# A first load of 128 descriptors, cut into four transfers over interleaved partitions (split GELU times x2)

## The chip, the cores and the metric

The kernel runs on one core of one Trainium2 chip. The metric is device time in microseconds (us) of one execution. Before the change it is 469.26 us, the median of three runs that lie between 469.24 and 469.31 us. A profile of one execution has a span of 467.9 us, from the first to the last instruction of the core; the execution that was profiled took 469.19 us. Times inside the kernel are counted from the start of that span.

## What is computed

The input has 32 x 512 rows of 2048 float32 values. In each row the first 1024 values go through the exact GELU and are multiplied by the other 1024.

```python
batch, seq, dim = (32, 512, 2048)
x1, x2 = (x[..., :half_dim].copy(), x[..., half_dim:].copy())
gelu_x1 = 0.5 * x1 * (1 + erf(x1 / np.sqrt(2)))
return (gelu_x1 * x2).astype(np.float32)
```

So 134.22 MB are read from HBM and 67.11 MB are written to it.

## The kernel before

A tile is 128 partitions of `R = 8` rows each, 8 MB of input and 4 MB of output; there are 16 tiles, and two buffers for each side. Partition `p` of a tile holds eight neighbouring rows, so a whole tile is one run of 64 KB per partition in HBM and in SBUF, and a half tile (four rows) one run of 32 KB. An engine that issues a transfer names the partitions and rows; one transfer becomes a list of descriptors, here one for each partition, which the core's 16 DMA engines work off.

```python
R = 8
x_t = x_flat.rearrange("(n p r) d -> n p r d", p=P, r=R)
x_bufs = [nc.alloc_sbuf_tensor(f"x{k}_tile", [P, R, dim], x.dtype) for k in range(2)]
o_bufs = [nc.alloc_sbuf_tensor(f"o{k}_tile", [P, R, half], out.dtype) for k in range(2)]
first = [nc.alloc_semaphore(f"first{j}") for j in range(2)]
# ...
def load(i, rows, sem):
    ins = nc.sync.dma_start(out=x_bufs[i % 2][:, rows, :], in_=x_t[i][:, rows, :])
    counted(ins, sem, 16)
    return ins
```

Three loads are issued by SyncE ahead of everything else: tile 0 in two halves, each with a semaphore of its own, and tile 1 whole. They are not put off behind the barrier that `tc.close()` ends with.

```python
for ins in (
    load(0, slice(0, 4), first[0]),
    load(0, slice(4, 8), first[1]),
    load(1, slice(0, 8), ready[1]),
):
    tc.no_tile_sem_insts.add(ins.ins.name)
tc.close()
```

Then, for each tile, ScalarE waits for the load, computes the GELU of the first half of each row into the output buffer, and VectorE multiplies it by the other half. The first and the last tile go in pieces of 2, 2 and 4 rows, the others in 5 and 3. The store is issued by ScalarE's queue (the last ones by SyncE's), and the load of tile `i + 2` by SyncE as soon as tile `i` has been multiplied. A load and the store of the same buffer number share the semaphore `ready[k]`, which ScalarE waits for two tiles later.

```python
for i in range(n_tiles):
    k = i % 2
    # ...
    for lo, hi in steps:
        rows = slice(lo, hi)
        if i == 0 and lo % 4 == 0:
            nc.scalar.wait_ge(first[lo // 4], 16)
        elif lo == 0:
            nc.scalar.wait_ge(ready[k], n[ready[k].name])
        # ScalarE: activation GELU; VectorE: tensor_mul; stores
    # ...
    if i + 2 < n_tiles:
        nc.sync.wait_ge(mul_done, n[mul_done.name])
        load(i + 2, slice(0, R), ready[k])
```

Of the kernel before, what the change touches and what calls it, by code (L numbers as in the profile page):

```python
# [1 line left out]

# [4 lines left out]

GELU = mybir.ActivationFunctionType.Gelu


@with_exitstack
def kernel(
    ctx: ExitStack,
    tc: tile.TileContext,
    x: bass.AP,
    out: bass.AP,
):
    nc = tc.nc
    P = nc.NUM_PARTITIONS

    x_flat = x.flatten_outer_dims()
    out_flat = out.flatten_outer_dims()
    n_rows, dim = x_flat.shape
    half = dim // 2

    R = 8
    x_t = x_flat.rearrange("(n p r) d -> n p r d", p=P, r=R)
    o_t = out_flat.rearrange("(n p r) d -> n p r d", p=P, r=R)
    n_tiles = x_t.shape[0]
# [6 lines that stand above are left out]
    ready = [nc.alloc_semaphore(f"ready{k}") for k in range(2)]  # L36
    gelu_done = nc.alloc_semaphore("gelu_done")
    mul_done = nc.alloc_semaphore("mul_done")
    tail_stored = nc.alloc_semaphore("tail_stored")
    n = {sem.name: 0 for sem in [*first, *ready, gelu_done, mul_done, tail_stored]}  # L40

    def counted(ins, sem, by):
        ins.then_inc(sem, by)
        n[sem.name] += by

    def load(i, rows, sem):
        ins = nc.sync.dma_start(out=x_bufs[i % 2][:, rows, :], in_=x_t[i][:, rows, :])  # L47
        counted(ins, sem, 16)
        return ins

    def store(queue, i, rows, sem):
        queue.wait_ge(mul_done, n[mul_done.name])
        counted(
            queue.dma_start(out=o_t[i][:, rows, :], in_=o_bufs[i % 2][:, rows, :]), sem, 16
        )

    for ins in (  # L60
        load(0, slice(0, 4), first[0]),
        load(0, slice(4, 8), first[1]),
        load(1, slice(0, 8), ready[1]),
    ):
        tc.no_tile_sem_insts.add(ins.ins.name)
    tc.close()
    tc.compile()  # L67

    for i in range(n_tiles):
        k = i % 2  # L70
        last = i == n_tiles - 1
        pieces = i == 0 or last
        steps = ((0, 2), (2, 4), (4, 8)) if pieces else ((0, 5), (5, 8))
        for lo, hi in steps:
            rows = slice(lo, hi)
            if i == 0 and lo % 4 == 0:
                nc.scalar.wait_ge(first[lo // 4], 16)
            elif lo == 0:
                nc.scalar.wait_ge(ready[k], n[ready[k].name])
            counted(  # L80
                nc.scalar.activation(  # L81
                    out=o_bufs[k][:, rows, :], in_=x_bufs[k][:, rows, :half], func=GELU
                ),
                gelu_done,
                1,
            )
            nc.vector.wait_ge(gelu_done, n[gelu_done.name])
            counted(
                nc.vector.tensor_mul(  # L89
                    out=o_bufs[k][:, rows, :],  # L90
                    in0=o_bufs[k][:, rows, :],
                    in1=x_bufs[k][:, rows, half:],
                ),
                mul_done,
                1,
            )
            if pieces and hi % 4 == 0:
                if last:
                    store(nc.sync, i, slice(hi - 4, hi), tail_stored)
                else:  # L100
                    store(nc.scalar, i, slice(hi - 4, hi), ready[k])
        if not pieces:
            if i == n_tiles - 2:
                store(nc.sync, i, slice(0, R), tail_stored)
            else:
                store(nc.scalar, i, slice(0, R), ready[k])
# [5 lines that stand above are left out]
    nc.scalar.drain()  # L112
    for sem in (*first, *ready):
        nc.scalar.sem_clear(sem)
    nc.vector.drain()
    nc.vector.sem_clear(gelu_done)
    nc.sync.sem_clear(mul_done)
    nc.sync.wait_ge(tail_stored, n[tail_stored.name]).then_inc(
        tail_stored, -n[tail_stored.name]
    )  # L120


# [1 line left out]
_INS = ['x']  # L124
_OUTS = [((32, 512, 1024), 'float32')]


# [23 lines left out]
```

## Time and profile before

| what | value |
|---|---|
| time, median of 3 | 469.26 us |
| span of the profile | 467.9 us |
| VectorE busy | 140.5 us (30%) |
| ScalarE busy | 115.5 us (25%) |
| DMA, mean over the span | 430 GB/s, 201.34 MB in 5041 packets |
| SyncE's queue (q1) | 2880 packets, 142.61 MB, 70.6% of 16 engines' span |
| ScalarE's queue (q10) | 2160 packets, 58.72 MB, 29.1% of 16 engines' span |
| issue of one of the first three loads | 383 to 425 ns |
| issue to landing of the first half tile | 12.0 us |
| first GELU starts at | 12.76 us |

How to read it: a page and its views give, for the core, the busy time of each engine, the DMA's share and rate in slices of the span, and the chain of waits that ended last. The window view cuts the span into stretches: each line has the length of the stretch, the busy time and number of instructions of VectorE (DVE), ScalarE (ACT) and GpSimd (POOL), a clock that does not matter here, the DMA share (1.00 is all 16 DMA engines busy) and the rate. In short windows a packet is counted whole where it starts, so the share can be over 1 in one and 0 in the next; the bytes of a window, divided by the size of a packet, count the packets that start in it. In the packet counts, each transfer of 128 descriptors has 128 data packets and 16 small ones that tell of its landing, so 144 in all.

### The profile page before, as it was taken

What the parts mean: (1) busy time and instruction counts of PE and PEld (TensorE: products, weight loads), DVE (VectorE), ACT (ScalarE), POOL (GpSimd) and SP (SyncE); (2) the same over time, 40 slices, a digit from 0 to 9 for tenths busy, and PEclk for the clock granted to TensorE, in tenths of its full rate; (3) what the DMA queues carried; (4) which work ended last, traced back from release to release, by engine and by line L of the source; (5) the groups of instructions that cost most, each with busy time, mean ns of one, the idle gap of its engine ahead of it and who ended that gap; (6) DMA issues with size and microseconds to landing.
All of it is one profiled execution on the core that took longest, in us unless ns stands there. A gap on an engine that the chain in (4) does not pass through costs nothing.

```text
span 467.9 us, 152 instructions
## 1 busy us (share of the span) xinstructions
DVE 140.5 (30%) x34; ACT 115.5 (25%) x35; POOL 0.2 (0%) x4
## 2 busy tenths in 40 slices
DVE  0330514207052060511606116060150702507043
ACT  1320606042060410604106050050500506014060
POOL 0000000000000000000000000000000000000000
DMA  8999999999999999999999999999999999999998
GB/s 359 448 448 443 403 405 492 409 403 448 459 437 403 434 417 493 403 403 448 476 420 403 445 406 493 403 406 445 487 409 403 445 451 448 403 434 417 493 389 373
DMA packets 5041, 201.34 MB, mean 430 GB/s; under 512 B 560, under 2 KB 560, under 8 KB 560
## 3 DMA queue, kind: packets, MB, share of 16 engines
q1 hardware_dynamic: 2880, 142.61, 70.6%
q10 hardware_dynamic: 2160, 58.72, 29.1%
q14 instruction: 1, 0.01, 0.0%
HBM read 134.22 MB, written 67.11 MB: 430 GB/s over the span
## 4 chain that ended last, share of the span: by engine, by line
DMA 76%; DVE 14%; ACT 8%; ACTq 0%; SPq 0%; issue 0%
DMA out_dram<-o_tile 66%; DVE o_tile L89 14%; DMA x_tile<-in_x_dram 10%; ACT o_tile L81 8%; ACTq L112 0%; SPq L47 0%
## 5 line engine op out<-in xcount | busy, mean ns | idle before, releaser
L89 DVE TENSOR_TENSOR o_tile<-o_tile,x_tile 128x5120 f32<-128x5120 f32 (+3 forms) x34 | 140.5, 4171 | 319.7 <-ACT o_tile L81 319.7
L81 ACT ACTIVATE o_tile<-x_tile 128x5120 f32<-128x5120 f32 (+3 forms) x34 | 114.3, 3407 | 337.4 <-DMA out_dram<-o_tile 301.6
L81 ACT ACT_TABLE_LOAD x1 | 1.3, 1283 | 2.9 <-PEq L67 2.9
L135 POOL MEMSET const-bfloat16-1.0<- 128x1 bf16 x1 | 0.1, 101 | 0.0
L135 POOL MEMSET const-uint8-127<- 128x1 uint8 x1 | 0.1, 101 | 0.0
L135 POOL MEMSET const-float32-0.0<- 128x1 f32 x1 | 0.1, 98 | 0.2 <-issue 0.2
L135 POOL MEMSET const-float32-1.0<- 128x1 f32 x1 | 0.1, 98 | 0.0
## 6 DMA issues: line engine op xcount, KB each, us to landing
out_dram<-o_tile ACTq DMA_DIRECT2D x13, 4096.0 KB, 44.7
x_tile<-in_x_dram SPq DMA_DIRECT2D x2, 4096.0 KB, 16.6
out_dram<-o_tile ACTq DMA_DIRECT2D x2, 2048.0 KB, 34.5
out_dram<-o_tile SPq DMA_DIRECT2D x1, 4096.0 KB, 25.2
out_dram<-o_tile SPq DMA_DIRECT2D x2, 2048.0 KB, 7.8
x_tile<-in_x_dram SPq DMA_DIRECT2D x15, 44.2
```

What stands on the lines that cost most here:

```text
L81: nc.scalar.activation(out=o_bufs[k][:, rows, :], in_=x_bufs[k][:, rows, :half], func=GELU),
L89: nc.vector.tensor_mul(out=o_bufs[k][:, rows, :], in0=o_bufs[k][:, rows, :], in1=x_bufs[k][:, rows, half:],),
L135: nc = _bacc.Bacc("TRN2", target_bir_lowering=False, num_devices=1)
```

## The change

The first half tile is loaded by four transfers, over the partitions 0, 8, 16, ... (16 of them), 4, 12, 20, ... (16), 2, 6, 10, ... (32) and 1, 3, 5, ... (64). Each partition is in exactly one of them, and each still is one descriptor of 32 KB. All four count on the same semaphore, so ScalarE waits for 64 in place of 16. It is for the start of the kernel: the DMA engines are to get their first descriptors from a short list, and the rest of the list is to be made while they work.

```diff
-    def load(i, rows, sem):
-        ins = nc.sync.dma_start(out=x_bufs[i % 2][:, rows, :], in_=x_t[i][:, rows, :])
+    first_parts = (slice(0, P, 8), slice(4, P, 8), slice(2, P, 4), slice(1, P, 2))
+
+    def load(i, rows, sem, parts=slice(0, P)):
+        ins = nc.sync.dma_start(out=x_bufs[i % 2][parts, rows, :], in_=x_t[i][parts, rows, :])
         counted(ins, sem, 16)
         return ins
@@
     for ins in (
-        load(0, slice(0, 4), first[0]),
+        *(load(0, slice(0, 4), first[0], parts) for parts in first_parts),
         load(0, slice(4, 8), first[1]),
         load(1, slice(0, 8), ready[1]),
     ):
@@
             if i == 0 and lo % 4 == 0:
-                nc.scalar.wait_ge(first[lo // 4], 16)
+                nc.scalar.wait_ge(first[lo // 4], n[first[lo // 4].name])
```

## The prediction

> **What bounds the kernel now.** I read the page first: the slices of the span, then the queues, then the chain of waits.
>
> ```profile
> span 467.9 us, 152 instructions
> DVE 140.5 (30%) x34; ACT 115.5 (25%) x35; POOL 0.2 (0%) x4
> DMA  8999999999999999999999999999999999999998
> q1 hardware_dynamic: 2880, 142.61, 70.6%
> q10 hardware_dynamic: 2160, 58.72, 29.1%
> DMA 76%; DVE 14%; ACT 8%; ACTq 0%; SPq 0%; issue 0%
> ```
>
> VectorE and ScalarE are idle for most of the time, and the DMA row is 9 in every slice but the first and the last. The two queues together hold the 16 DMA engines for 70.6 + 29.1 = 99.7% of the span. The chain gives 22% to VectorE and ScalarE only because it runs through them: while they work, the queues go on moving bytes. So the kernel is as long as the DMA engines need, and only three things count: when they start, whether they ever pause or slow down, and when they end.
>
> How near the floor is that? In the window view, the long middle stretch runs at full share and 432 GB/s:
>
> ```profile
> 0.00:1.74 1.74, 0.00 (x0) 0.00 (x0) 0.20 (x4) 1.00 0.00 0
> ...
> 100.00:400.00 300.00, 92.55 (x21) 78.35 (x22) 0.00 (x0) 1.00 1.00 432
> ```
>
> 201.33 MB at 432 GB/s are 466.0 us; 467.9 - 466.0 leaves 1.9 us, and the first line shows that 1.74 us of it pass before any packet starts. There is hardly a pause to remove behind the start. What is left to win is in that lead and in the first packets.
>
> **The start in detail.** Windows of 0.2 us over the first packets (the last two numbers of a line are the DMA share and GB/s):
>
> ```profile
> 1.40:1.60 0.20, 0.00 (x0) 0.00 (x0) 0.00 (x0) 1.00 0.00 0
> 1.60:1.80 0.20, 0.00 (x0) 0.00 (x0) 0.00 (x0) 1.00 2.27 655
> 1.80:2.00 0.20, 0.00 (x0) 0.00 (x0) 0.00 (x0) 1.00 4.66 1311
> 2.00:2.20 0.20, 0.00 (x0) 0.00 (x0) 0.00 (x0) 1.00 1.69 492
> 2.20:2.40 0.20, 0.00 (x0) 0.00 (x0) 0.00 (x0) 1.00 0.50 164
> ...
> 3.40:3.60 0.20, 0.00 (x0) 0.20 (x1) 0.00 (x0) 1.00 1.14 492
> 3.60:3.80 0.20, 0.00 (x0) 0.20 (x1) 0.00 (x0) 1.00 2.27 983
> 3.80:4.00 0.20, 0.00 (x0) 0.20 (x1) 0.00 (x0) 1.00 2.65 1147
> ```
>
> A packet of 32 KB counts as 164 GB/s in a window of 0.2 us. So 4, 8, 3 and 1 packets start in the four windows from 1.60 to 2.40: sixteen, one for each DMA engine, strung out over 0.6 us or so. The share gives their length: (2.27 + 4.66 + 1.69 + 0.50) x 0.2 us x 16 / 16 packets = 1.82 us each. The next wave starts between 3.40 and 4.00 (3 + 6 + 7 packets); its share gives (1.14 + 2.27 + 2.65) x 0.2 = 1.21 us each, and all later waves of the half tile look the same. So the first packet of an engine costs 0.61 us more than a steady one, and the engines are out of step by up to 0.6 us. As nothing pauses later, the engine that is last here stays late to the end.
>
> [...] No run so far shows a transfer over strided partitions.
>
> **The change, part by part.**
>
> *Issues.* One issue goes, four come. The old ones took 383 to 425 ns; three more delay what follows on SyncE by about 3 x 0.43 = 1.3 us. The second half tile is then issued at some 1.16 + 1.3 = 2.5 us and tile 1 at 2.9 us. The engines first need them after the eight waves of the first half, at about 12 us, so this is hidden. The same goes for the barrier behind the issues: the table load of ScalarE moves from 2.86 to about 4.2 us, and the first GELU waits until 12.76 us.
>
> *Feeding.* The first short list gives an engine one packet, to about 3.5 us. The second list is issued some 0.45 us after the first, the third and fourth 0.9 and 1.3 us after it; at the old 1.0 us from issue (0.73) to first packet (1.74) they are ready at 2.2, 2.6 and 3.1 us. They hold one, two and four more packets per engine, so no engine runs dry.
>
> *Landing packets.* Three more per engine, in a place where each has a share of 9 ns or less; 0.03 us at most, an estimate.
>
> *The first wave, where the gain is.* If the 0.6 us by which the sixteen starts differ come from making 128 descriptors, 16 of them should do it in an eighth: starts within about 0.1 us of each other. The last engine would gain up to 0.4 us, the mean one 0.2 us. The 0.61 us of extra length in the first packet look like the time to the first data, which a shorter list does not remove. I put the gain at 0.3 us, less 0.03: 469.26 - 0.27 = 469.0 us.
>
> [...] Eight waves would then take 2.42 us in place of 1.21: 8 x 1.21 = 9.7 us lost, less about a tenth[...]: 8.7 us. That gives 478 us. All of it would be on the path, since the DMA engines are the bound.
>
> **The rivals.**
> - *A short list starts the engines together[...]* (0.57). For it: the strung-out starts, no pause later. The partitions are also interleaved[...] and each prefix of the four lists is even. Time 468.6 to 469.2.
> - [...] (0.27). [...] Time 476 to 479.
> - [...] (0.08): two to four waves doubled, 2.4 to 4.8 us, so 471 to 474.
> - *Nothing is gained* (0.08): the starts differ for another reason than the length of the list, or the second list comes late to some engines. Time 469.2 to 469.7.
>
> **Range and chances.** The likeliest single outcome is 469.0 us. The outcomes lie in two heaps, at 469 and at 477; a range that holds 8 in 10 has to reach into the second, so I give 468.5 to 478.0. A gain over 2% (9.4 us) is not to be had, since only 1.9 us are not steady transfer. [...] So faster 0.01, within 2% 0.95, slower 0.04.
>
> **What would show each step right or wrong.** Windows of 0.2 us from 1.4 to 4.0 us: sixteen starts within one or two windows confirm the feeding step; the same spread refutes it. [...] Issue to landing of the first half tile: about 12 us or a little less in one case, near 20 us in the other, and the first GELU at 12.5 or at 21 us with it. The rate in the middle stretch should stay at 432 GB/s; if it changes, something other than the start is at work and the prediction is wrong in a way that it does not foresee.

## The result, and the profile after

The changed kernel takes 471.36 us (six runs, 471.27 to 471.47) beside 469.25 us (median of six) for the kernel before: a ratio of 1.0044, 95% interval 1.0031 to 1.0057. It is 2.1 us slower. The page of the changed kernel, in the lines that answer to those shown of the kernel before:

```profile
span 469.9 us, 155 instructions
DVE 140.5 (30%) x34; ACT 115.6 (25%) x35; POOL 0.2 (0%) x4
DMA  8999998999999999999999999999999999999989
q1 hardware_dynamic: 2928, 142.61, 70.7%
q10 hardware_dynamic: 2160, 58.72, 29.0%
DMA 75%; DVE 14%; ACT 8%; SPq 1%; ACTq 0%; issue 0%
```

The bound has not moved: the same bytes, the same two queues, 70.7 + 29.0 = 99.7% of the span again. 48 packets have come to SyncE's queue, the landing packets of three more transfers. What an average over the span cannot show is the start, so I cut it such that each window holds one wave, sixteen packets, as many as there are DMA engines. As a packet counts where it starts, share times length of the window is then the mean length of a packet, landing packets (the small ones that tell of a transfer's landing) included. The window view of the changed kernel (the last two numbers are the DMA share and GB/s):

```profile
0.00:2.10 2.10, 0.00 (x0) 0.00 (x0) 0.20 (x4) 1.00 0.00 0
2.10:4.00 1.90, 0.00 (x0) 0.00 (x0) 0.00 (x0) 1.00 1.23 276
4.00:6.00 2.00, 0.00 (x0) 0.88 (x1) 0.00 (x0) 1.00 1.20 262
6.00:8.00 2.00, 0.00 (x0) 0.41 (x1) 0.00 (x0) 1.00 0.83 262
8.00:9.50 1.50, 0.00 (x0) 0.00 (x0) 0.00 (x0) 1.00 0.81 350
9.50:10.50 1.00, 0.00 (x0) 0.00 (x0) 0.00 (x0) 1.00 1.23 524
```

and of the kernel before, cut in the same way:

```profile
1.60:3.00 1.40, 0.00 (x0) 0.14 (x1) 0.00 (x0) 1.00 1.30 374
3.00:4.50 1.50, 0.00 (x0) 1.14 (x1) 0.00 (x0) 1.00 0.81 350
4.50:5.50 1.00, 0.00 (x0) 0.00 (x0) 0.00 (x0) 1.00 1.21 524
```

Wave by wave, mean length of a packet of 32 KB:

| wave | list in the changed kernel | before | after | lost |
|---|---|---|---|---|
| 1 | 16, partitions 0, 8, ... | 1.82 us | 2.34 us | 0.52 us |
| 2 | 16, partitions 4, 12, ... | 1.21 us | 2.40 us | 1.19 us |
| 3 | 32, first packet | 1.21 us | 1.66 us | 0.45 us |
| 4 | 32, second packet | 1.21 us | 1.22 us | 0 |
| 5 on | 64 | 1.21 us | 1.23 us | 0 |

Wave 2 is the plain case: twice the length, and in the trace all sixteen packets of it take between 2.37 and 2.39 us. In wave 1 part of the doubling may be hidden behind what makes the first packets long in the kernel before as well (1.82 us); no run takes the two apart. Wave 3 is slow too: in the trace its packets take 1.89 us where they start first and 1.41 us where they start last. Engines still at work on wave 2 are at most part of the reason, as the last packet of wave 3 starts when wave 2 has just ended (7.41 us). The table sums to 2.16 us. To it comes a later start: the mean first packet starts at 2.26 us, not 1.92 (from the packets of the two traces), 0.34 us. (Five runs below also begin with the one list of 128 partitions; in their traces the mean is 1.96 to 2.02 us, so the later start is worth 0.24 to 0.34 us.) Together that is 2.5 us, and the first GELU starts 2.65 us later:

```profile
15.41 3.71 ACT L85 ACTIVATE o_tile<-x_tile 128x2048 f32<-128x2048 f32 x2 [9.00 <-DMA x_tile<-in_x_dram]
```

Not all of it reaches the end, which is 2.1 us later. The first wave of tile 1 (64 KB each) was slow in the kernel before, 2.70 us per packet, and is not in the changed one, 2.70 x 0.90 = 2.43 us, so 0.27 us come back there:

```profile
21.50:22.50 1.00, 0.00 (x0) 0.04 (x1) 0.00 (x0) 1.00 2.70 1049
```

```profile
24.10:25.00 0.90, 0.00 (x0) 0.00 (x0) 0.00 (x0) 1.00 2.70 1165
```

The first of these lines is of before, the second of after; each window has the sixteen packets of that wave. Why that wave has a cost in one and not in the other is not settled.

### The profile page after: what moved, and what is told of

Its sections match the earlier page's. It is cut to its first block, busy times and chain, and to the rows that moved or that the text cites. A ratio compares the mean times of both kernels' runs of the same rounds, so it can differ in the third digit from the quotient of the medians.

```text
span 469.9 us, 155 instructions
## 1 busy us (share of the span) xinstructions
DVE 140.5 (30%) x34; ACT 115.6 (25%) x35; POOL 0.2 (0%) x4
## 3 DMA queue, kind: packets, MB, share of 16 engines
q1 hardware_dynamic: 2928, 142.61, 70.7%
## 4 chain that ended last, share of the span: by engine, by line
DMA 75%; DVE 14%; ACT 8%; SPq 1%; ACTq 0%; issue 0%
DMA out_dram<-o_tile 66%; DVE o_tile L93 14%; DMA x_tile<-in_x_dram 10%; ACT o_tile L85 8%; SPq L51 1%; ACTq L116 0%
```

## Theories

**A, partitions.** The time of a packet depends on the partitions to which the packets under way at the same time go: some sets of partitions lengthen their packets, others do not. Call it a meeting when two packets lengthen each other in this way. Which packets meet was my assumption, and no trace shows a meeting as such: in a list of 16 with stride 8 each packet was to meet one other and take twice 1.21 us, in lists of 16 neighbours more of them, in lists of 32 with stride 4 and of 64 with stride 2 none. **B, transfers.** Each transfer more has a price: a longer issue, landing packets, an engine left without work. **C, the start.** Short lists are bad only where the engines have nothing else queued. **D, HBM.** The runs of a list of 16 lie 512 KB apart in HBM, and that distance is what is slow. **E, sixteen.** A list of 16 partitions with a stride is slow as such, whichever partitions they are; this rival was set up last, with the lists of stride 7.

## Experiments on the lists

**Three lists, none of 16.**

```diff
-first_parts = (slice(0, P, 8), slice(4, P, 8), slice(2, P, 4), slice(1, P, 2))
+first_parts = (slice(0, P, 4), slice(2, P, 4), slice(1, P, 2))
```

> Three lists (32, 32 and 64 partitions, strides 4, 4 and 2) in place of four; no list of 16. Theory A [...]: all packets of the first half tile after the first wave take about 1.21 us, none 2.4; only the later first packet (some 0.4 us after that of the kernel before) is left, so 469.3 to 469.7 us. Theory B (each transfer more costs about 0.7 us, by its longer issue, its landing packets or a starved engine): two transfers more in place of three, 470.5 to 470.8 us.

Measured: 469.72 us, ratio 1.0006 (0.9998 to 1.0014). The windows of its first three waves:

```profile
0.00:2.04 2.04, 0.00 (x0) 0.00 (x0) 0.20 (x4) 1.00 0.00 0
2.04:3.50 1.46, 0.00 (x0) 0.00 (x0) 0.00 (x0) 1.00 1.29 359
3.50:5.00 1.50, 0.00 (x0) 0.47 (x1) 0.00 (x0) 1.00 0.82 350
5.00:6.00 1.00, 0.00 (x0) 0.82 (x1) 0.00 (x0) 1.00 1.22 524
```

1.29 x 1.46 = 1.88 us, then 1.23 and 1.22 us: no doubled wave. With three transfers in place of four, 1.6 of the 2.1 us are gone; B would have kept 1.2 to 1.5. The late start (nothing before 2.04 us) has stayed.

**Eight lists of 16.**

```diff
+first_parts = (slice(0, P, 8), slice(4, P, 8), slice(2, P, 8), slice(6, P, 8),
+               slice(1, P, 8), slice(5, P, 8), slice(3, P, 8), slice(7, P, 8))
```

> Eight lists of 16, each with stride 8. Theory A: all eight waves take about 2.4 us per packet; 8 x 1.21 us less some overlap are lost, 477 to 479 us, and the first half tile lands about 9 us later than in the kernel before. Theory B (0.7 us per transfer more, seven more than before): 474.2 us, with packets of 1.2 us and pauses between them.

Measured: 478.23 us, ratio 1.0192 (1.0178 to 1.0206). By its windows the first wave takes 2.34 us per packet and the other seven 2.38 to 2.40; the third to the fifth:

```profile
6.00:8.00 2.00, 0.00 (x0) 0.38 (x1) 0.00 (x0) 1.00 1.20 262
8.00:10.00 2.00, 0.00 (x0) 0.90 (x1) 0.00 (x0) 1.00 1.19 262
10.00:12.50 2.50, 0.00 (x0) 0.00 (x0) 0.00 (x0) 1.00 0.96 210
```

2.40, 2.38 and 2.40 us, without a pause between them, as A has it and not B (1.2 us with pauses). Eight doubled waves cost 8.9 us.

**The same lists, long ones first.**

```diff
+first_parts = (slice(1, P, 2), slice(2, P, 4), slice(0, P, 8), slice(4, P, 8))
```

> The same four lists in the order 64, 32, 16, 16. Theory A: the doubled packets (2.4 us) move with the lists of 16 to the end of the half tile, the six waves ahead of them take 1.21 us; loss about as in the changed kernel or a little more, 471.2 to 472.0 us, and the residue falls on the second half tile's first wave. Theory C (the loss is one of the start: short lists come too slowly for engines that have nothing else to do): with the list of 64 first nothing is lost, 469.3 us.

Measured: 471.74 us, ratio 1.0055 (1.0042 to 1.0067). Waves 6 to 9 (the last of the list of 32, the two lists of 16, the first of the second half tile) in its windows:

```profile
8.50:9.50 1.00, 0.00 (x0) 0.00 (x0) 0.00 (x0) 1.00 1.21 524
9.50:11.00 1.50, 0.00 (x0) 0.00 (x0) 0.00 (x0) 1.00 1.35 350
11.00:13.50 2.50, 0.00 (x0) 0.00 (x0) 0.00 (x0) 1.00 0.94 210
13.50:15.50 2.00, 0.00 (x0) 0.00 (x0) 0.00 (x0) 1.00 0.83 262
```

1.21, 2.03, 2.35 and 1.66 us. The slow waves move with the lists of 16, to a place behind six other waves, 9.5 us and more from the start, and still cost 0.82 + 1.14 + 0.45 = 2.4 us. So the loss is not one of the start, and C is refuted.

**Neighbouring partitions in lists of the same sizes.**

```diff
+first_parts = (slice(0, 16), slice(16, 32), slice(32, 64), slice(64, P))
```

> Lists of 16, 16, 32 and 64 neighbouring partitions, as many transfers of the same sizes as in the changed kernel. Theory A: [...] packets of the first two lists take about 4.8 us (7 us lost in place of 2.4), and the lists of 32 and 64 [...] their six waves take at least 2.4 us each (7 us more): 483 us[...]. Theory B: as the changed kernel, 471.4 us.

Measured: 483.17 us, ratio 1.0297 (1.0281 to 1.0313). The first five waves (16, 16, 32, 32, 64 neighbours):

```profile
1.50:4.00 2.50, 0.00 (x0) 0.00 (x0) 0.00 (x0) 1.00 1.54 210
4.00:8.00 4.00, 0.00 (x0) 1.28 (x1) 0.00 (x0) 1.00 1.14 131
8.00:12.00 4.00, 0.00 (x0) 0.00 (x0) 0.00 (x0) 1.00 0.77 131
12.00:15.00 3.00, 0.00 (x0) 0.00 (x0) 0.00 (x0) 1.00 0.85 175
15.00:17.20 2.20, 0.00 (x0) 0.00 (x0) 0.00 (x0) 1.00 1.12 238
```

The second wave, of 16 neighbours, takes 4.56 us per packet; the second wave of the 32 neighbours and the first of the 64 take 2.55 and 2.46 us (waves 4 and 5). Waves 1 and 3, the first of all and the first behind the change from 16 to 32 neighbours, take 3.85 and 3.08 us. The number of transfers and their sizes are those of the changed kernel, so B (471.4 us) falls here for good. Another point lies in the first window: a list of 16 that is a run of neighbours has its first packets spread from 1.77 to 2.44 us, by the trace, while the list of 128 had them from 1.74 to 2.30. So a short list does not as such bring the first packets closer together. The spread also differs from profile to profile: 0.76 to 0.97 us for the same list of 128 in the five runs with an extra load below, 0.41 us for the first list of 16 in the run with eight lists.

## Experiments on partitions and HBM apart

Here the first load is the old one, and an extra load into an output buffer that is not in use yet stands between the two halves of tile 0; it brings bytes that are not used for the result. In the first two runs a second extra load stands behind the second half. ScalarE waits for the extra loads as well. Partitions and HBM runs are chosen apart.

```diff
+    x_all = x_flat.rearrange("(q r) d -> q r d", r=R)
+    def probe(k, parts, source):      # 32 KB per partition, counted on first[k]
+        ...dma_start(out=o_bufs[k][parts, ...], in_=x_all[source, 0:4, :]...)
         load(0, slice(0, 4), first[0]),
+        probe(0, slice(0, P, 8), slice(512, 528)),      # 16 partitions, neighbouring runs
         load(0, slice(4, 8), first[1]),
+        probe(1, slice(0, 106, 7), slice(528, 544)),
```

> The kernel before, with two extra loads of 16 descriptors of 32 KB into output buffers that are not yet in use: one to the partitions 0, 8, ..., 120 but from neighbouring runs in HBM (64 KB apart), one to the partitions 0, 7, ..., 105, also from neighbours. Theory A [...]: the first has 16 packets of about 2.4 us; in the second [...] about four packets are near 2.4 us and twelve near 1.2 us. Theory D (it is the distance of 512 KB between the runs in HBM): all 32 packets take 1.2 us. Time: 469.3 plus 2.4 plus up to 2.4 us, so 473 to 474 us by A; 471.7 us by D.

Measured: 474.14 us, ratio 1.0106 (1.0092 to 1.0120). The last wave of the first half, the first extra load and what follows it:

```profile
10.50:11.50 1.00, 0.00 (x0) 0.00 (x0) 0.00 (x0) 1.00 1.21 524
11.50:13.00 1.50, 0.00 (x0) 0.00 (x0) 0.00 (x0) 1.00 1.36 350
13.00:15.50 2.50, 0.00 (x0) 0.00 (x0) 0.00 (x0) 1.00 0.65 210
```

2.04 us in the list, and 1.63 us in the wave behind it: 0.83 + 0.42 = 1.25 us lost, about one packet's length (1.21 us), though its runs in HBM are neighbours; by D these packets would have taken 1.21 us. By itself this does not decide between A and E, since a list of stride 7 loses nearly as much (1.09 us, below). The second extra load came when ScalarE had just issued the first store (22.06 us), so I leave it aside; it was tried again alone, below.

```diff
+        probe(0, slice(0, P, 4), slice(512, 768, 8)),   # 32 partitions, runs 512 KB apart
+        probe(1, slice(0, 61, 4), slice(768, 784)),
```

> The same with two other extra loads: 32 descriptors to the partitions 0, 4, ..., 124 from runs 512 KB apart in HBM, and 16 descriptors to the partitions 0, 4, ..., 60 from neighbouring runs. Theory A: the first has packets of 1.2 us in both waves[...]; the second [...] its 16 packets take about 2.4 us. Theory D: the first takes 2.4 us per packet, the second 1.2 us. Time: 469.3 + 2.4 + 2.4 = 474.1 us by A, 469.3 + 4.8 + 1.2 = 475.3 us by D.

Measured: 473.81 us, ratio 1.0098 (1.0084 to 1.0111). Both waves of the first extra load:

```profile
11.50:13.00 1.50, 0.00 (x0) 0.00 (x0) 0.00 (x0) 1.00 0.81 350
13.00:14.20 1.20, 0.00 (x0) 0.00 (x0) 0.00 (x0) 1.00 1.01 437
```

1.21 us each, at 512 KB between runs. The second extra load again met the first store and is left aside. The counterpart has the same runs in HBM and 32 neighbouring partitions:

```diff
+        probe(0, slice(0, 32), slice(512, 768, 8)),
```

> The same with 32 descriptors to the neighbouring partitions 0 to 31, from runs 512 KB apart in HBM. Theory A: [...] both waves take about 2.4 to 2.6 us per packet, twice those of the list to every fourth partition from the same runs (1.21 us); about 2.4 us more than an unhindered list, 469.3 + 2.4 + 2.4 = 474.1 us. Theory D (the distance in HBM): 1.21 us, as there, and 471.7 us. The issue: near 0.4 us if it is the stride on the SBUF side that lengthens it, near 0.57 us if it is that in HBM.

Measured: 474.15 us, ratio 1.0107 (1.0090 to 1.0124).

```profile
11.50:13.00 1.50, 0.00 (x0) 0.00 (x0) 0.00 (x0) 1.00 1.36 350
13.00:15.50 2.50, 0.00 (x0) 0.00 (x0) 0.00 (x0) 1.00 1.03 210
15.50:17.90 2.40, 0.00 (x0) 0.00 (x0) 0.00 (x0) 1.00 0.76 218
```

2.04 and 2.58 us, and 1.82 us in the wave behind. Same source, same size, same queue: only the partitions differ from the list that ran at 1.21 us. So D is refuted, and for these two lists of 32 the cause is on the SBUF side.

**Which packets are slowed?** For a list with stride 7 my assumption by A was that only two pairs of packets meet; no run had shown it.

```diff
+        probe(0, slice(0, 106, 7), slice(512, 528)),
```

> The kernel before with one extra load, between the two halves of tile 0, of 16 descriptors of 32 KB to the partitions 0, 7, ..., 105 from neighbouring runs in HBM; nothing else is in the queues then. Theory A: [...] most of the sixteen packets take 1.2 to 1.5 us [...] and about four 2.4 to 2.9 us. Rival (any list of 16 with a stride is slow as such): sixteen packets of about 2 us, as with stride 8.

Measured: 471.20 us, ratio 1.0041 (1.0026 to 1.0056). The list and the wave behind it:

```profile
11.50:13.00 1.50, 0.00 (x0) 0.00 (x0) 0.00 (x0) 1.00 1.23 350
13.00:15.00 2.00, 0.00 (x0) 0.00 (x0) 0.00 (x0) 1.00 0.83 262
```

1.85 and 1.66 us on average, and by the trace no packet of the list is under 1.58 or over 2.07. A expected most of them near 1.2 and four near 2.4; it missed, and E, with about 2 us, came closer. Over both waves 0.64 + 0.45 = 1.09 us are lost, against 1.25 us with stride 8. Seven such lists in a row were to tell whether only the packets that A expects to meet are slowed, or all:

```diff
+        *(probe(0, slice(c, c + 106, 7), slice(512 + 16 * c, 528 + 16 * c)) for c in range(7)),
```

> The kernel before with seven extra loads of 16 descriptors in a row between the two halves of tile 0, to the partitions c, c + 7, ..., c + 105 with c from 0 to 6, from neighbouring runs in HBM. [...] If only engines that meet are slowed [...], about ten packets of sixteen stay at 1.21 us and the others go up to 2.4 us and more, mean 1.4 to 1.9 us, and the engines drift apart by several us. If a meeting slows all engines alike, all sixteen packets of a wave are equally long, near 1.6 to 2.1 us, and the engines stay together within 1 us. If a list of 16 with a stride is slow as such, they take 2.4 us like those of stride 8.

Measured: 484.99 us, ratio 1.0307 (1.0258 to 1.0356), with more scatter than any other (483.33 to 487.10; the profile is of the slowest). Lists one to seven:

```profile
11.50:13.00 1.50, 0.00 (x0) 0.00 (x0) 0.00 (x0) 1.00 1.28 350
13.00:15.50 2.50, 0.00 (x0) 0.00 (x0) 0.00 (x0) 1.00 0.91 210
15.50:17.50 2.00, 0.00 (x0) 0.00 (x0) 0.00 (x0) 1.00 1.11 262
17.50:20.00 2.50, 0.00 (x0) 0.00 (x0) 0.00 (x0) 1.00 0.74 210
20.00:21.80 1.80, 0.00 (x0) 0.00 (x0) 0.00 (x0) 1.00 1.11 291
21.80:23.80 2.00, 0.00 (x0) 0.00 (x0) 0.00 (x0) 1.00 1.08 262
23.80:26.00 2.20, 0.00 (x0) 0.00 (x0) 0.00 (x0) 1.00 0.99 238
```

1.92, 2.28, 2.22, 1.85, 2.00, 2.16 and 2.18 us on average, and within a list the packets differ by 0.8 us at most. No packet is under 1.59 us, where a steady one takes 1.21, so all sixteen packets of a list are slowed, not the two or four that A expected.

So A's estimates come close for lists of 128, of 32 with stride 4 and of 64 with stride 2 (1.21 to 1.23 us), for 16 with stride 8 (2.4 us expected, 2.35 to 2.40 measured behind another such wave), for 16 neighbours (4.8 and 4.56 us) and for 32 and 64 of them (2.4 us and more, and 2.55 and 2.46 us), but not for 16 with stride 7. E is not excluded for the strided lists of 16, those of the changed kernel among them: it expected about 2 us for the single list and 2.4 us for the seven, and the means lie at 1.85 to 2.28. It does not account for 4.56 us with 16 neighbours, nor for 2.5 us with 32 and 64 of them. A strided list of 16 with packets of 1.21 us would refute E; no run here shows one. Why the lists with stride 7 are slow in all their packets is open; the trace does not say which engine moved which packet.

## Experiments on the start

```diff
+first_parts = (slice(0, P, 2), slice(1, P, 2))
```

> Two lists of 64 partitions (the even, then the odd ones). Theory A: no doubled packets, 469.3 to 469.8 us. If the long issue (0.55 to 0.60 us in place of 0.38) and the late first packet (2.1 in place of 1.74 us) belong to a list with a stride, both are seen here too, and the time is that of the three lists of 32, 32 and 64 (469.7 us); if they belong to having many transfers in a row, the first issue is back at about 0.4 us and the time at 469.3 us.

Measured: 469.72 us, ratio 1.0011 (1.0004 to 1.0017). The issues of the two lists, and the first wave:

```profile
L51 SPq DMA_DIRECT2D x_tile<-in_x_dram x2: 542/558/575, 0.7 to 1.3; - x2
```

```profile
0.00:2.04 2.04, 0.00 (x0) 0.00 (x0) 0.20 (x4) 1.00 0.00 0
2.04:3.50 1.46, 0.00 (x0) 0.00 (x0) 0.00 (x0) 1.00 1.23 359
```

Two strided lists alone show the long issue (542 ns at least, against 383) and the late first packet. The lists of neighbours were issued in 393 to 413 ns, and their first packet came at 1.77 us. The extra load to neighbours from runs 512 KB apart took 419 ns to issue, the one to a stride of 8 from neighbouring runs 566 ns:

```profile
L63 SPq DMA_DIRECT2D o_tile<-in_x_dram x1: 419/419/419, 1.2 to 1.2; - x1
```

```profile
L63 SPq DMA_DIRECT2D o_tile<-in_x_dram x1: 566/566/566, 1.2 to 1.2; - x1
```

So it is a stride over SBUF partitions, not one in HBM, that lengthens these issues. It is not all that does: in the run with lists of neighbours the fourth and fifth issue took 531 and 587 ns without any stride, and an issue of 128 partitions right behind a strided one took 627 ns. The first packet comes 0.3 to 0.4 us later where the first list is strided; there the runs in HBM are strided too, and the two were not tried apart for it.

One more run splits the first load of the kernel before by rows, not by partitions, and `load` takes the queue as an argument:

```diff
-        load(0, slice(0, 4), first[0]),
+        load(0, slice(0, 2), first[0]),
+        load(0, slice(2, 4), first[0], nc.scalar),
```

> The first half tile as two transfers of all 128 partitions, two rows each, one issued by SyncE and one by ScalarE at the same time; all else as before. If the strung-out first packets come from how one queue hands out its list, a second queue lets late engines start on the other one, and 0.1 to 0.4 us are won: 468.9 to 469.2 us. If they come from the engines themselves, it stays at 469.3 us. Theory A has no doubled packets here.

Measured: 469.27 us, ratio 0.9997 (0.9988 to 1.0005): nothing won. The first packets of 16 KB still start over 1.1 us, from 1.75 to 2.84 us. The first packets of the second half tile start over 0.43 us (12.15 to 12.58 us), beside 0.47 us in the kernel before. No version tried here is faster than the kernel before.

## Why the prediction was right and wrong

The measured 471.36 us lies in the range of 468.5 to 478.0 us, but that is luck: the range was stretched from one heap of outcomes, at 469 us, to the other, at 477 us, and the result fell between them, in a rival that was given 0.08. The point, 469.0 us, and the likeliest rival, a small gain, were wrong.

- *What bounds the kernel*: right. 99.7% of the span is DMA before and after, and a loss at the start came through to the end but for 0.4 us.
- *How near the floor*: the rate of 432 GB/s, and with it the 1.9 us that are not steady transfer, is less firm than it was taken for. A window counts packets where they start, so its rate depends on where it is cut: the same window of the changed kernel reads 435 GB/s, although its packets of 64 KB take 2.42 us there as before. At the 434 GB/s of the window from 22 to 100 us of the kernel before, 4.0 us would be left. The prediction called another rate there a sign of a foreign cause; here it is none.

```profile
100.00:400.00 300.00, 90.52 (x21) 78.36 (x22) 0.00 (x0) 1.00 1.01 435
```

- *Issues, feeding, landing packets*: the order was right, as no engine ran dry and wave 2 follows wave 1 at once. An issue of a strided list was put at 0.43 us and takes 0.57 to 0.60; that is hidden for the later ones, but not for the first. This is the term for which I took the old 1.0 us from issue to first packet: it is 1.39 us (0.73 to 2.12).
- *The first wave, where the gain is*: **this step failed.** It said that a list of 16 makes the starts coincide and wins 0.3 us. Fifteen of the sixteen do start within 0.24 us, between 2.12 and 2.36 us, but one starts at 3.02, and taken in order each is later than its counterpart before (windows of the changed kernel with 7, 8 and 1 packets):

```profile
2.00:2.20 0.20, 0.00 (x0) 0.00 (x0) 0.00 (x0) 1.00 4.92 1147
2.20:2.40 0.20, 0.00 (x0) 0.00 (x0) 0.00 (x0) 1.00 6.15 1311
3.00:3.20 0.20, 0.00 (x0) 0.00 (x0) 0.00 (x0) 1.00 0.62 164
```

The spread is not a matter of the length of the list alone, since 16 neighbours show it as well (0.67 us). The term is a loss of 0.24 to 0.34 us in place of a gain of 0.3. What the spread comes from stays open.

- *Doubled waves, where the loss may be*: that a wave could take twice its time was my assumption, shown by no run at that point. The doubled waves came for the lists of 16, and they were given too little weight (0.27 and 0.08 in two rivals). The size was right: the 8.7 us put down for eight doubled waves were 8.9 us with eight lists of 16, the later start included. That all eight waves double failed: steady packets of the lists of 32 and 64 with strides 4 and 2 take 1.21 to 1.23 us. The third rival, given 0.08, with two to four doubled waves, has the right waves and the right time: it said 2.4 us at the least, and 2.16 us are lost in packets. Why a strided list of 16 is slow is not shown: A misses the lists of stride 7, and no run takes it apart from E for the lists of stride 8.
- *What spoke for the gain*: that the partitions were interleaved evenly. It was no evidence: a list of 16 with stride 8 is even over the partition numbers, and its packets take 2.35 to 2.40 us behind another such list.

## What to carry to other kernels

Before a transfer is cut by partitions, time the packets of each piece, and do not count only the packets or descriptors: in this kernel, bound by DMA, pieces of 16 partitions with stride 8 took 2.35 to 2.40 us per packet, one piece behind another, in place of 1.21, and with two such pieces 2.1 us stayed lost at the end. Another stride was no safeguard (1.85 to 2.28 us with stride 7). If it must be cut, pieces of 32 with stride 4 or 64 with stride 2 kept 1.21 to 1.23 us per packet behind the first wave here, at the price of a first packet that is later by 0.3 us (2.04 us in place of 1.74). And a spread of first packets at the start is not by itself a sign that the list is too long.

## What the runs showed of the hardware

- A packet of 32 KB, sixteen of them under way at a time, takes 1.21 to 1.23 us behind the first wave in lists of 128 partitions, of 32 with stride 4 and of 64 with stride 2; 1.21 us is 27.1 GB/s for each packet. In the first wave behind slower lists it takes 1.63 to 1.96 us. It takes 2.35 to 2.40 us in a list of 16 with stride 8 behind another such list, and 2.03 to 2.04 us in one that follows waves of 1.21 us. In lists of neighbours it takes 4.56 us in the second list of 16, and 2.55 and 2.46 us in the list of 32 (its second wave) and of 64 (its first); 32 neighbours behind waves of 1.21 us take 2.04 and 2.58 us.
- In lists of 16 with stride 7 it takes 1.85 to 2.28 us on average (single packets 1.58 to 2.38 us), and all sixteen packets are slowed; why is not shown.
- A first issue on SyncE takes 542 to 602 ns with a stride over SBUF partitions and 371 to 397 ns without; 512 KB between runs in HBM alone leaves an issue at 419 ns. Later issues can take as long without a stride (531 to 587 ns, run with lists of neighbours).
